# Two PSUM banks for the transposes between the stages of a two-block transformer, and an urgent half of the modulation

## The chip, the cores and the metric

The kernel runs on one core of a Trainium2 chip, in one launch. The metric is the device time of an execution in microseconds. A core has five engines that each work through their own fixed list of instructions: TensorE (PE: matmuls and transposes; PEld is its loading of weights), VectorE (DVE), ScalarE (ACT), GpSimd (POOL) and SyncE (SP, which issues the loads). They wait for each other by semaphores. Matmul results land in PSUM, which has eight banks of 2 KB for each of 128 partitions.

## What is computed

Two blocks over 256 tokens of 1024 features, in float32. The first is an mLSTM mixer (with a context of 256 more tokens) followed by a gated convolution MLP; the second has two layers, each with three sublayers: feed-forward, mixer (gated linear attention in the first layer, latent attention in the second), feed-forward. What concerns this change is how every sublayer begins: the tokens are normalised and each feature is scaled and shifted by numbers that depend on the conditioning vector `c`.

```python
def rmsnorm_2(x, g):
    xf = x.astype(jnp.float32)
    y = xf * lax.rsqrt(jnp.mean(xf * xf, axis=-1, keepdims=True) + EPS)
    return (y * g.astype(jnp.float32)).astype(x.dtype)

def swiglu(h, w_gu, w_down):
    gate, up = jnp.split(h @ w_gu, 2, axis=-1)
    return (jax.nn.silu(gate) * up) @ w_down

def sublayer(x, shift, scale, gate, g_pre, g_post, fn, res_weight):
    h = rmsnorm_2(x, g_pre) * (1 + scale[:, None, :]) + shift[:, None, :]
    return x + res_weight * gate[:, None, :] * rmsnorm_2(fn(h), g_post)
```

## The kernel before

Tokens are worked on in two halves of 128, called t = 0 and t = 1 here, features in eight groups of 128. The weights (340 MB of traffic in all) are streamed from HBM once, 512 KB at a time (`raw`), and every float32 product is made of three matmuls: each operand is split into a rounded part and its remainder, and `mm3` (lines 250 to 252) sums hi x hi, hi x lo and lo x hi. For a weight ScalarE makes the rounded part (`whi`, line 236, or `wA`, `wB`, `wC` where it has a place of its own) and VectorE the remainder (`wlo`, line 237). For the activations ScalarE makes `u_hi` and VectorE `u_lo` (`hilo`, lines 245 and 246). VectorE also works off a queue of background products of the conditioning vector with weights (`gjunk`, line 256).

Between two stages stands this chain, once for each token half: the squares are summed (ScalarE, `ajunk`, line 324), VectorE forms the root in some five small operations (lines 298 to 311), and scales the tokens to `xn` (line 370, or 908 at the start of the first feed-forward). In `modulated` TensorE transposes `xn` by groups of four features into one PSUM bank (`pt`, line 347, tag `tc`); for the first four groups VectorE applies scale and shift (`u`, line 358), for the last four ScalarE does (line 362); then each half of `u` is split into `u_hi` and `u_lo`. The bank holds one half: the transposes of the second half wait until the first four modulations have read it. `modulated` is called 16 times: twice each at the start of the gated convolution MLP, the four feed-forwards apart from the one at the layer boundary, the gated linear attention and the latent attention, and four times at the boundary of the two layers, where two differently modulated copies are made of each token half.

The tag `tr` of the same pool is a second bank with one buffer. The feed-forward uses it for the transposes of its product `h_` (`pt2`, line 966), the helper `row_of` for a row vector, the attention parts for their own transposes.

The program is written as a plain sequence; a scheduler sorts each engine's list at build time by its own estimate of when things are ready and by priority. `urgent(offset)` raises the priority of what is issued in it: the ends of stages are written inside such blocks (`with urgent(uo(t)): fin(t, acc)`), with matmuls of the stage that ends or of the other token half as work to put between. So an edit in `modulated` can move instructions that it doesn't name. In the feed-forward the order of chunk products is a list (`FFN_ORDER`), whose accumulators are `acc`, and whose up products land in `mm`.

Of the kernel before, what the change touches and what calls it, by code (L numbers as in the profile page):

```python
# [7 lines left out]
F32 = mybir.dt.float32  # L8
# [4 lines left out]
ALU = mybir.AluOpType  # L13
# [97 lines left out]
def kernel(ctx: ExitStack, tc: tile.TileContext, a: dict, out: bass.AP):  # L111
    nc = tc.nc
    V, S, T, G = nc.vector, nc.scalar, nc.tensor, nc.gpsimd

    def pool(name, bufs, **kw):
        return ctx.enter_context(tc.tile_pool(name=name, bufs=bufs, **kw))
# [14 lines left out]
    ps_tr = pool("ps_tr", 1, space=PSUM)  # L131

    def urgent(offset=1500):
        return tc.high_priority(offset=offset)
# [109 lines left out]
    def hilo(hi, lo, src):  # L244
        mark["ehi"] = S.copy(hi, src)  # L245
        mark["elo"] = V.tensor_tensor(out=lo, in0=src, in1=hi.bitcast(F32), op=ALU.subtract)  # L246
        return mark["elo"]
# [95 lines left out]
    def t4(src, h, pt=None):  # L343
        if pt is None:
            pt = ps_tr.tile([128, 4, 128], F32, name="pt", tag="tc")
        for k in range(4):
            T.transpose(pt[:, k, :], src[:, (h * 4 + k) * 128:(h * 4 + k + 1) * 128], ident)  # L347
        return pt

    def modulated(xn, gs, sh, uh, ul):  # L350

        for h in range(2):
            ks = slice(h * 4, h * 4 + 4)
            pt = t4(xn, h)
            u = wk.tile([128, 4, 128], F32, name="u", tag="u")
            if h == 0:
                for k in range(4):
                    V.tensor_scalar(out=u[:, k, :], in0=pt[:, k, :], scalar1=gs[:, k:k + 1], scalar2=sh[:, k:k + 1],
                                    op0=ALU.mult, op1=ALU.add)
            else:  # L360
                for k in range(4):
                    S.activation(out=u[:, k, :], in_=pt[:, k, :], func=AF.Identity,
                                 scale=gs[:, 4 + k:5 + k], bias=sh[:, 4 + k:5 + k])
            hilo(uh[:, ks, :], ul[:, ks, :], u)
# [8 lines left out]
    def prenorm(src, gs, sh, t):  # L373
        ts = slice(t * 128, t * 128 + 128)
        xn = normed(src)
        modulated(xn, gs, sh, u_hi[:, :, ts], u_lo[:, :, ts])
        return xn
# [508 lines left out]
    def fin_glu(t, acc):  # L886
        ga2, gfin = rows1
        y = wk.tile([128, D], F32, name="y", tag="xn")
        ss = sm.tile([128, 8], F32, name="ssf", tag="ssf", bufs=2)
        for h, v in enumerate(halves(y)):  # L890
            s = slice(h * 512, h * 512 + 512)
            V.tensor_tensor(out=v, in0=acc[h], in1=ga2[:, s], op=ALU.mult)
            V.tensor_tensor(out=v, in0=x[:, t, s], in1=v, op=ALU.add)
            mean_square(v, ss[:, h:h + 1], D)
        z = x[:, t, :]
        for h, v in enumerate(halves(y)):
            w = z[:, h * 512:h * 512 + 512]
            V.tensor_tensor(out=w, in0=v, in1=gfin[:, h * 512:h * 512 + 512], op=ALU.mult)
            mean_square(w, ss[:, 2 + h:3 + h], D)
        V.tensor_scalar(out=ss[:, 4:5], in0=ss[:, 0:1], scalar1=ss[:, 1:2], scalar2=0.5 * EPS, op0=ALU.add, op1=ALU.add)  # L900
        V.tensor_scalar(out=ss[:, 5:6], in0=ss[:, 2:3], scalar1=ss[:, 3:4], scalar2=None, op0=ALU.add)
        r = rsqrt_half(ss[:, 4:5])
        V.tensor_scalar(out=ss[:, 6:7], in0=ss[:, 5:6], scalar1=r, scalar2=r, op0=ALU.mult, op1=ALU.mult)
        V.tensor_scalar(out=ss[:, 6:7], in0=ss[:, 6:7], scalar1=0.5 * EPS, scalar2=None, op0=ALU.add)
        r2 = rsqrt_half(ss[:, 6:7])
        xn = wk.tile([128, D], F32, name="xn", tag="xn")
        for v, w in zip(halves(xn), halves(z)):
            V.tensor_scalar(out=v, in0=w, scalar1=r, scalar2=r2, op0=ALU.mult, op1=ALU.mult)
        ts = slice(t * 128, t * 128 + 128)
        modulated(xn, mod2[:, 1, :], mod2[:, 0, :], u_hi[:, :, ts], u_lo[:, :, ts])  # L910
        V.tensor_scalar_mul(out=z, in0=z, scalar1=r)
# [275 lines left out]
    def mla_u(t, xn):  # L1187

        if t == 0:
            mla.u = second()  # L1190
        ts = slice(t * 128, t * 128 + 128)
        modulated(xn, mod2[:, 19, :], mod2[:, 18, :], mla.u[0][:, :, ts], mla.u[1][:, :, ts])
# [310 lines left out]
```

## Time and profile before

| | |
|---|---|
| median of 3 runs | 1437.48 us (1434.57 to 1437.93) |
| the profiled execution | 1434.38 us |
| its span, first to last instruction | 1432.6 us |
| mean granted clock of TensorE | 0.986 of full |
| TensorE busy | 1380.0 us, 96% |
| VectorE busy | 1113.9 us, 78% |
| ScalarE busy | 720.5 us, 50% |
| data moved | 340.24 MB, 238 GB/s in the mean |

In the rows further down, a line of the timeline gives an operation's start and its length in microseconds, engine and source line, what it writes and reads, how many are taken together (x4), and in brackets how long the engine had been idle before it and what ended that. A waiting row gives the engine that waited, the instruction it waited at, what it waited for, and the sum, the number and the longest of such waits. Matmuls overlap: each takes 0.39 us at full clock though the next starts 0.23 us after it.

### The profile page before, as it was taken

The page shows a single profiled execution, that of the slowest core. Times are in us where ns is not written, and L with a number is a line of the kernel's source. Part 1 is how long each engine was busy: PE and PEld are TensorE (multiplying, and loading weights), DVE is VectorE, ACT ScalarE, POOL GpSimd, SP SyncE. Part 2 cuts the span into 40 slices and gives each one's busy share as a digit, 9 for nine tenths or more (in the row PEclk, how much of TensorE's full clock was granted, in tenths as well). Part 3 has the DMA queues.
Part 4 walks back from the last instruction along what each step waited for, and adds up shares of the span by engine and source line. Part 5 has one row for each costly group of instructions (what it writes and reads, how often), then busy time and mean ns, then how long its engine had stood idle before and what let it go on. Part 6 is the DMA issues. An engine that isn't in the chain of part 4 may idle for free.

```text
span 1432.6 us, 22526 instructions
## 1 busy us (share of the span) xinstructions
PE 1380.0 (96%) x8425; PEld 1204.0 (84%) x8425; DVE 1113.9 (78%) x2115; ACT 720.5 (50%) x1188; POOL 18.2 (1%) x42
## 2 busy tenths in 40 slices
PE   6999999999989999999999999999999999899997
PEld 6978877899978999878678999879999776789996
DVE  6887788898688888689788888698878786756563
ACT  4634764545354545566454545554554666644451
POOL 1000000000000000000000000000000000000000
PEclk8999999999999999999999999999999999999999
DMA  8576446797528999568548999469889472366750
GB/s 330 203 265 234 162 151 234 264 323 272 184 96 290 336 340 345 196 222 290 187 154 289 341 335 344 147 202 334 317 310 333 138 253 80 121 198 205 276 170 30
DMA packets 94943, 340.24 MB, mean 238 GB/s; under 512 B 10928, under 2 KB 11248, under 8 KB 94832
## 3 DMA queue, kind: packets, MB, share of 16 engines
q1 hardware_dynamic: 92736, 332.47, 65.6%
q0 software_dynamic: 2096, 6.33, 1.5%
q8 instruction: 66, 1.08, 0.3%
q14 instruction: 45, 0.37, 0.1%
HBM read 337.67 MB, written 1.08 MB: 236 GB/s over the span
## 4 chain that ended last, share of the span: by engine, by line
PE 70%; DVE 11%; DMA 10%; ACT 4%; issue 3%; SPq 0%; DVEq 0%; ACTq 0%; POOLq 0%
PE mm L250 12%; PE mm L252 11%; PE mm L251 11%; PE acc L252 8%; PE acc L250 8%; PE acc L251 8%; DMA raw<-in_cond_w_dram 3%; DVE wlo L237 3%; DVE gjunk L256 2%; PE acc L733 2%; ACT whi L236 1%; ACT ajunk L324 1%; PE pt L347 1%; PE pg L556 1%; DMA row<-d 1%
## 5 line engine op out<-in xcount | busy, mean ns | idle before, releaser
L237 DVE TENSOR_TENSOR wlo<-raw,whi 128x1024 fp32r<-128x1024 f32 (+1 forms) x385 | 462.5, 1207 | 109.6 <-ACT whi L236 106.7
L236 ACT CAST whi<-raw 128x1024 fp32r<-128x1024 f32 (+1 forms) x385 | 395.7, 1038 | 277.1 <-PE mm L251 79.5
L250 PE MATMUL mm<-u_hi,whi 128*128 128x256 f32 x1384 | 388.5, 281 | 0.2 <-DVE hf L831 0.2
L251 PE MATMUL mm<-u_lo,whi 128*128 128x256 f32 x1384 | 386.6, 279 | 0.0
L252 PE MATMUL mm<-u_hi,wlo 128*128 128x256 f32 x1384 | 386.5, 279 | 0.0
L250 PEld LDWEIGHTS mm<-u_hi,whi 128*128 128x128 f32 x1384 | 260.0, 188 | 4.4 <-DVE hf L831 0.6
L251 PEld LDWEIGHTS mm<-u_lo,whi 128*128 128x128 f32 x1384 | 259.3, 187 | 3.3
L252 PEld LDWEIGHTS mm<-u_hi,wlo 128*128 128x128 f32 x1384 | 260.1, 188 | 0.0
L256 DVE CUSTOM_DVE_ANT_0 gjunk<-raw,c 128x1024 bf16<-128x1024 f32 x192 | 234.3, 1221 | 24.1 <-DMA raw<-in_cond_w_dram 16.5
L250 PE MATMUL acc<-whi,hh 128*128 128x512 f32 x388 | 153.6, 398 | 4.5 <-ACT hh L245 4.5
L252 PE MATMUL acc<-whi,hl 128*128 128x512 f32 x388 | 153.3, 397 | 0.3 <-DVE hl L246 0.3
L251 PE MATMUL acc<-wlo,hh 128*128 128x512 f32 x388 | 152.5, 393 | 0.5 <-DVE wlo L237 0.5
L252 PEld LDWEIGHTS acc<-whi,hl 128*128 128x128 f32 x388 | 73.4, 189 | 17.4 <-DVE hl L246 0.7
L250 PEld LDWEIGHTS acc<-whi,hh 128*128 128x128 f32 x388 | 72.9, 188 | 17.5 <-ACT hh L245 5.0
L252 PE MATMUL acc<-whi,u_lo 128*128 128x512 f32 (+1 forms) x216 | 86.7, 403 | 0.5 <-DVE u_lo L246 0.5
L250 PE MATMUL acc<-whi,u_hi 128*128 128x512 f32 (+1 forms) x216 | 86.5, 401 | 0.0
L251 PE MATMUL acc<-wlo,u_hi 128*128 128x512 f32 (+1 forms) x216 | 86.4, 400 | 0.0
L251 PEld LDWEIGHTS acc<-wlo,hh 128*128 128x128 f32 x388 | 73.2, 189 | 14.2 <-DVE wlo L237 1.3
L251 PE MATMUL mm<-wlo,u_hi 128*128 128x512 f32 x144 | 57.3, 398 | 0.0
L250 PE MATMUL mm<-whi,u_hi 128*128 128x512 f32 x144 | 57.2, 397 | 0.0
L252 PE MATMUL mm<-whi,u_lo 128*128 128x512 f32 x144 | 57.0, 397 | 0.0
L946 ACT ACTIVATE sg<-mm 128x256 f32<-128x256 f32 x64 | 24.3, 380 | 59.6 <-PE mm L252 59.5
(734 smaller groups left out, 1998.6 us busy)
## 6 DMA issues: line engine op xcount, KB each, us to landing
raw<-in_cond_w_dram SPq DMA_DIRECT2D x144, 512.0 KB, 5.2
raw<-in_gu_ws_dram SPq DMA_DIRECT2D x128, 512.0 KB, 5.0
raw<-in_dn_dram SPq DMA_DIRECT2D x88, 512.0 KB, 4.9
raw<-in_gu_dram SPq DMA_DIRECT2D x48, 512.0 KB, 4.3
raw<-in_w_mod_dram SPq DMA_DIRECT2D x32, 512.0 KB, 4.3
raw<-in_f_down_dram SPq DMA_DIRECT2D x22, 512.0 KB, 4.6
raw<-in_f_gate_dram SPq DMA_DIRECT2D x18, 512.0 KB, 4.9
raw<-in_a_vo_dram SPq DMA_DIRECT2D x16, 512.0 KB, 5.1
```

The source lines that it names most:

```text
L236: o1 = S.copy(hi[:, :n], r[:, :n])
L237: o2 = V.tensor_tensor(out=lo[:, :n], in0=r[:, :n], in1=hi[:, :n].bitcast(F32), op=ALU.subtract)
L250: T.matmul(ps, lhsT=lh, rhs=rh, start=first, stop=False)
L251: T.matmul(ps, lhsT=lh, rhs=rl, start=False, stop=False)
L252: T.matmul(ps, lhsT=ll, rhs=rh, start=False, stop=last)
L256: return V.tensor_tensor_reduce(out=junk, in0=r, in1=vec, scale=1.0, scalar=0.0, op0=ALU.mult, op1=ALU.add, accum_out=dst)
L324: mark["ms"] = S.activation(out=junk[:, :src.shape[-1]], in_=src, func=AF.Square, scale=float(2 * width) ** -0.5, accum_out=dst)
L347: T.transpose(pt[:, k, :], src[:, (h * 4 + k) * 128:(h * 4 + k + 1) * 128], ident)
L556: o = T.matmul(pg, lhsT=wsc[:, k * 128:k * 128 + 128], rhs=ccol[:, k, :], start=(k == 0), stop=(k == 7))
L733: T.matmul(np_[:, 0:257], lhsT=w[:, d, s, :], rhs=vt[s][:, h, :], start=(i == 0), stop=(i == len(tiles) - 1))
L946: S.activation(out=sg, in_=ps[:, 0:256], func=AF.Silu)
```

## The change

In `modulated` the transposes of both halves are issued first, the first half's into `tc` as before, the second half's into `tr`; VectorE's four modulations stand in `urgent(2500)`, above the offsets of 300 to 2000 used elsewhere in the kernel. Two lines are added, so line 358 of before is 360 after, 362 is 364, 908 is 910, and so on.

```diff
@@ -349,14 +349,16 @@
 
     def modulated(xn, gs, sh, uh, ul):
 
+        pts = [t4(xn, 0), t4(xn, 1, ps_tr.tile([128, 4, 128], F32, name="pt", tag="tr"))]
         for h in range(2):
             ks = slice(h * 4, h * 4 + 4)
-            pt = t4(xn, h)
+            pt = pts[h]
             u = wk.tile([128, 4, 128], F32, name="u", tag="u")
             if h == 0:
-                for k in range(4):
-                    V.tensor_scalar(out=u[:, k, :], in0=pt[:, k, :], scalar1=gs[:, k:k + 1], scalar2=sh[:, k:k + 1],
-                                    op0=ALU.mult, op1=ALU.add)
+                with urgent(2500):
+                    for k in range(4):
+                        V.tensor_scalar(out=u[:, k, :], in0=pt[:, k, :], scalar1=gs[:, k:k + 1], scalar2=sh[:, k:k + 1],
+                                        op0=ALU.mult, op1=ALU.add)
             else:
                 for k in range(4):
                     S.activation(out=u[:, k, :], in_=pt[:, k, :], func=AF.Identity,
```

The lists of SyncE and GpSimd stay as they are. Those of TensorE, VectorE and ScalarE move at every call. Three places follow, all at the start of the first feed-forward.

VectorE before, ahead of the second token half's norm result `xn` (four `wlo` stand between the previous half's `u_lo` and `xn`; `h__4310` is a product of the feed-forward that has begun on the first token half, `hl` its remainder):

```order
L308 SCALAR_TENSOR_TENSOR w<-w 128x1
L237 TENSOR_TENSOR wlo<-raw,whi 128x1024
L309 SCALAR_TENSOR_TENSOR r<-w,yi 128x1
L237 TENSOR_TENSOR wlo<-raw,whi 128x1024
L310 SCALAR_TENSOR_TENSOR w<-r,ssf 128x1
L237 TENSOR_TENSOR wlo<-raw,whi 128x1024
L311 SCALAR_TENSOR_TENSOR r<-w,r 128x1
L237 TENSOR_TENSOR wlo<-raw,whi 128x1024
L908 TENSOR_SCALAR xn<-x,r 128x512 x2
L963 TENSOR_TENSOR h__4310<-sg,mm 128x256
L911 TENSOR_SCALAR x<-x,r 128x1024
L358 TENSOR_SCALAR u<-pt,mod_118 128x128 x4
```

VectorE after, from that product on; five `wlo` stand already ahead of the first row here:

```order
L965 TENSOR_TENSOR h__4310<-sg,mm 128x256
L311 SCALAR_TENSOR_TENSOR r<-w,r 128x1
L256 ISA gjunk,mod_118<-raw,c_2574 128x1024
L256 ISA mod_118 128x1
L905 TENSOR_SCALAR ssf<-ssf,r 128x1
L237 TENSOR_TENSOR wlo<-raw,whi 128x1024
L906 TENSOR_SCALAR ssf<-ssf 128x1
L237 TENSOR_TENSOR wlo<-raw,whi 128x1024
L298 TENSOR_SCALAR yi<-ssf 128x1
L306 TENSOR_SCALAR w<-ssf 128x1
L307 SCALAR_TENSOR_TENSOR w<-yi,w 128x1
L237 TENSOR_TENSOR wlo<-raw,whi 128x1024
```

and straight on:

```order
L308 SCALAR_TENSOR_TENSOR w<-w 128x1
L965 TENSOR_TENSOR h__4370<-sg,mm 128x256
L309 SCALAR_TENSOR_TENSOR r<-w,yi 128x1
L310 SCALAR_TENSOR_TENSOR w<-r,ssf 128x1
L311 SCALAR_TENSOR_TENSOR r<-w,r 128x1
L910 TENSOR_SCALAR xn<-x,r 128x512 x2
L913 TENSOR_SCALAR x<-x,r 128x1024
L360 TENSOR_SCALAR u<-pt,mod_118 128x128 x4
```

Between the previous half's `u_lo` and `xn` are now eight `wlo`, one `gjunk` and the products `h__4310` and `h__4370`; before there were four `wlo` and nothing of the others.

TensorE before, around the two sets of transposes of the same token half (`mm` are up products of the first token half, `mm<-wA,u_hi` the first of the second):

```order
L252 MATMUL mm<-whi,u_lo 128x512
L347 MATMUL pt<-ident,xn 128x128 x4
L250 MATMUL mm<-whi,u_hi 128x512
L966 MATMUL pt_4312<-ident,h__4310 128x128 x2
L251 MATMUL mm<-wlo,u_hi 128x512
```

and, six matmuls on,

```order
L252 MATMUL mm<-whi,u_lo 128x512
L250 MATMUL mm<-whi,u_hi 128x512
L347 MATMUL pt<-ident,xn 128x128 x4
L250 MATMUL acc_4258<-whi,hh 128x512
L250 MATMUL acc_4259<-whi,hh 128x512
L250 MATMUL mm<-wA,u_hi 128x512
L251 MATMUL mm<-wA,u_hi 128x512
```

TensorE after, the same place:

```order
L250 MATMUL mm<-whi,u_hi 128x512
L251 MATMUL mm<-wlo,u_hi 128x512
L252 MATMUL mm<-whi,u_lo 128x512
L347 MATMUL pt<-ident,xn 128x128 x8
L968 MATMUL pt_4312<-ident,h__4310 128x128 x2
L250 MATMUL mm<-wA,u_hi 128x512
L251 MATMUL mm<-wA,u_hi 128x512
L250 MATMUL acc_4258<-whi,hh 128x512
L251 MATMUL acc_4258<-wlo,hh 128x512
L252 MATMUL mm<-wA,u_lo 128x512
```

The ten matmuls on `whi` that stood between the two sets, and five more that came behind the first of the new token half, are ahead of both; the feed-forward's transpose `pt_4312` follows the eight, and the first matmul of the new token half follows that.

ScalarE before, at the first token half (`ajunk` are sums of squares of the other half's norm):

```order
L236 CAST wC<-raw 128x1024
L236 CAST wA<-raw 128x1024
L324 ACTIVATE ajunk,ssf<-y 128x512 x2
L324 ACTIVATE ajunk,ssf<-x 128x512 x2
L245 CAST u_hi<-u 128x4x128
L362 ACTIVATE u<-pt,mod_118 128x128 x4
L245 CAST u_hi<-u 128x4x128
L236 CAST whi<-raw 128x1024 x5
```

ScalarE after, the same place:

```order
L236 CAST wC<-raw 128x1024
L364 ACTIVATE u<-pt,mod_118 128x128 x4
L245 CAST u_hi<-u 128x4x128 x2
L236 CAST wA<-raw 128x1024
L236 CAST whi<-raw 128x1024
L324 ACTIVATE ajunk,ssf<-y 128x512
L236 CAST whi<-raw 128x1024
L324 ACTIVATE ajunk,ssf<-y 128x512
```

The four modulations come before both casts of `u_hi`, and both of those before the sums of squares, which are now apart from each other with casts of weights between.

## Rows read from the trace of the kernel before

**Rows 1.** The page, busy time, share of the span and number of instructions.

```profile
PE 1380.0 (96%) x8425; PEld 1204.0 (84%) x8425; DVE 1113.9 (78%) x2115; ACT 720.5 (50%) x1188; POOL 18.2 (1%) x42
```

**Rows 2.** Waits of TensorE: us in total, times, longest us.

```profile
PE pt L347 <- DVE u L358: 8.6, 6, 3.6
...
PE pt L347 <- DVE xn L370: 5.1, 4, 2.4
...
PE mm L250 <- ACT u_hi L245: 0.2, 1, 0.2
```

**Rows 3.** Timeline, start of the gated linear attention, second token half.

```profile
622.47 0.66 PE L347 MATMUL pt<-ident,xn 128*128 128x128 f32 x4 [0.81 <-DVE xn L370]
623.16 1.36 DVE L358 TENSOR_SCALAR u<-pt,mod 128x128 f32<-128x128 f32 x4 [0.35 <-PE pt L347]
...
624.56 0.62 ACT L245 CAST u_hi<-u 128x512 fp32r<-128x512 f32 x1 [1.50 <-DVE u L358]
...
624.58 0.66 PE L347 MATMUL pt<-ident,xn 128*128 128x128 f32 x4 [1.46 <-DVE u L358]
...
625.23 0.58 PE L250 MATMUL mm<-u_hi,whi 128*128 128x256 f32 x1
625.27 1.51 ACT L362 ACTIVATE u<-pt,mod 128x128 f32<-128x128 f32 x4
...
628.07 2.35 DVE L237 TENSOR_TENSOR wlo<-raw,whi 128x1024 fp32r<-128x1024 f32 x2
```

**Rows 4.** Timeline, first feed-forward, first token half: VectorE, then TensorE.

```profile
413.03 1.04 DVE L358 TENSOR_SCALAR u<-pt,mod 128x128 f32<-128x128 f32 x3
414.05 1.38 DVE L892 TENSOR_TENSOR y<-acc,row 128x512 f32<-128x512 f32 x2
...
417.87 0.40 DVE L358 TENSOR_SCALAR u<-pt,mod 128x128 f32<-128x128 f32 x1
...
418.31 1.21 DVE L237 TENSOR_TENSOR wA<-raw,wA 128x1024 fp32r<-128x1024 f32 x1
...
418.32 1.12 PE L347 MATMUL pt<-ident,xn 128*128 128x128 f32 x4 [3.63 <-DVE u L358]
...
420.19 0.63 PE L251 MATMUL mm<-wA,u_hi 128*128 128x512 f32 x1
```

**Rows 5.** Windows: TensorE's busy us (instructions), granted clock, share of DMA, GB/s.

```profile
418.00:421.00 3.00, 2.52 (x7) 0.50 0.14 34
421.00:425.00 4.00, 4.00 (x13) 0.66 0.36 119
...
625.00:628.00 3.00, 3.00 (x11) 0.52 0.39 137
...
1234.00:1237.00 3.00, 2.93 (x9) 0.50 0.02 5
```

**Rows 6.** Timeline, first feed-forward, second token half: VectorE, ScalarE, TensorE.

```profile
427.50 1.00 DVE L908 TENSOR_SCALAR xn<-x,r 128x512 f32<-128x512 f32 x2
428.41 0.41 DVE L963 TENSOR_TENSOR h__4310<-sg,mm 128x256 f32<-128x256 f32 x1
...
434.06 1.22 DVE L256 CUSTOM_DVE_ANT_0 gjunk<-raw,c 128x1024 bf16<-128x1024 f32 x1
...
429.85 1.05 ACT L236 CAST whi<-raw 128x1024 fp32r<-128x1024 f32 x1 [2.10 <-DMA raw<-in_dn_dram]
...
429.27 0.60 PE L347 MATMUL pt<-ident,xn 128*128 128x128 f32 x4
...
431.10 0.40 PE L252 MATMUL mm<-whi,u_lo 128*128 128x512 f32 x1
431.34 0.39 PE L250 MATMUL mm<-whi,u_hi 128*128 128x512 f32 x1
...
432.26 0.60 PE L347 MATMUL pt<-ident,xn 128*128 128x128 f32 x4
```

**Rows 7.** Timeline of TensorE, last feed-forward, first token half.

```profile
1234.07 1.11 PE L347 MATMUL pt<-ident,xn 128*128 128x128 f32 x4 [1.52 <-DVE u L358]
```

## The prediction

> **What bounds the kernel now.** I read the busy line of the page first: TensorE works 1380.0 of 1432.6 us [rows 1], so only its 52.6 us of idle time and the stretches at half clock can move the end. Then I asked for the waits of TensorE. Two of its groups belong to this code: the second set of transposes (line 347) waited for VectorE's modulations `u` (line 358) six times, 8.6 us in all, 3.6 us the longest, and the first set waited for the norm's result `xn` four times, 5.1 us. The matmuls waited for ScalarE's cast `u_hi` once, 0.2 us [rows 2]. The 8.6 us are everything that a second bank can take away directly, 0.6% of the span. Then I looked at single places in the timeline.
>
> A stage begins so, in the gated attention's second half of the tokens [rows 3]: four transposes at 622.47, VectorE's four modulations from 623.16 (1.36 us), TensorE idle for 1.46 us, the other four transposes at 624.58 (they need the bank that VectorE has just emptied), beside them the cast `u_hi` of the first half (0.62 us), and at 625.23 the first matmul. From the first transpose to the first matmul are 2.76 us. ScalarE's modulations of the second half (1.51 us) come only then. The first matmul takes features from the first half, so the first cast decides.
>
> The longest wait stands at the start of the first feed-forward layer, first token half [rows 4]: VectorE runs three modulations from 413.03, then six operations of the other token half's norm (lines 892, 893 and 898, from 414.05 on), and only then the fourth at 417.87. TensorE resumes at 418.32. Its matmul of line 251 there, at 420.19, needs VectorE's `wA` (418.31 to 419.5).
>
> The windows give the granted clock behind such waits [rows 5]: 0.50 from 418 to 421 (the lower of the two levels, 1.2 GHz), a mixture of both to 425 at 0.66, 0.52 from 625 to 628, 0.50 from 1234 to 1237. Busy time at a clock c holds c as much work, so the place at 418 cost 2.52 x 0.50 + 4.00 x 0.34 = 2.6 us, that at 625 3.00 x 0.48 = 1.4 us, and that at 1234 2.93 x 0.50 = 1.5 us in this window.
>
> **What the change does at any site.** It adds no instruction and no transfer; the order of SyncE and GpSimd does not move, so no load is issued elsewhere in the program. Eight transposes go back to back and take 1.2 us (0.66 for four, 0.13 more for each of the next four [rows 3]). VectorE and ScalarE then modulate at the same time, from different banks. What is late next is ScalarE: in its fixed order the four modulations of half 1 stand ahead of both casts, as the order of ScalarE in the section on the change shows for the first feed-forward start. So the first matmul comes at 1.2 + 1.51 + 0.62 = about 3.4 us from the first transpose, where before it came at 2.76: 0.65 us later, though the second half's features are there 1 us earlier. An idle TensorE is not idle for less; its wait goes over from `u` to `u_hi`. Where matmuls of the old stage stand between, the 3.4 us are covered if there are nine or more of them (2.1 us beside the 1.2 us of transposes).
>
> The Trainium skill (Perfetto Trace Analysis, Matmuls) says that independent groups should rotate through different PSUM banks so that the evacuation of one overlaps the next group's matmuls. By that rule alone the 8.6 us would go, and the time would be the gain rival's below. The trace here shows what stands behind the bank, a cast on an engine that has just been given two jobs ahead of it.
>
> **First feed-forward start, first token half.** The fourth modulation now follows the third, at 414.05, and the 3.63 us stall in front of the transposes goes. But VectorE still owes six norm operations (3.8 us, from 414.05 to the fourth modulation [rows 4]), two `u_lo` (half a `wlo` in elements, some 0.6 us each) and `wA` (1.15), in that order: 414.4 + 3.8 + 1.2 + 1.15 = 420.5 us. The matmul of line 251 needs that and started at 420.19 before. I take +0.3 us; the bounds are -3.6 (the whole wait goes) and +1.
>
> **First feed-forward start, second token half.** This is the largest term. Before, VectorE had four `wlo` between the `u_lo` and this half's `xn`, which ran from 427.50 to 428.4, and TensorE reached the transposes at 429.27 without waiting [rows 6]. After, by VectorE's order, eight `wlo`, one `gjunk` and the two products `h__4310` and `h__4370` stand ahead of `xn`: 4 x 1.13 + 1.15 + 2 x 0.35 = 6.4 us more (the second `wlo` of a pair adds 1.13 of 2.35 [rows 3]; `gjunk` and `h` by rows 6, less the overlap of some 0.07), so `xn` is whole at about 434.8. It can be later: the last of these `wlo` need feed-forward weights whose `whi` casts ScalarE could start only at 429.85, after waiting 2.10 us for the transfer; two more at some 2 us each make it 437. TensorE meanwhile has run out: the ten matmuls on `whi` that stood between the two sets of transposes and five that came soon after are now all ahead of the first (429.27 + 15 x 0.23 = 432.7, the pitch by rows 6; with the 0.3 from above 433.0). That is a hole of 1.8 us, 4 if the transfers bind; I take the first. Behind it the eight transposes, then at once the feed-forward's own transpose `pt_4312`, whose bank is now the one that ScalarE empties, and the first matmul: 3.4 less 1.3 = 2 us more that nothing covers, where before there was no gap at all. Two holes so near each other have gone with half clock at each of the three places of rows 5, at 1.4 to 2.6 us each; I count 2.5. Sum 1.8 + 2 + 2.5 = +6.3 us, bounds 0 (VectorE runs ahead of what I think) and +9.
>
> **Gated attention start.** First token half: TensorE's order has only three matmuls after the eight transposes, then a feed-forward transpose that waits for ScalarE's modulations, and the first projection; before, seven stood between the sets and a gap of 0.25 us was all. I take +1.4. Second half: `xn` as before; 0.65 us later by the site rule, less the 0.81 us that TensorE waited for `xn` [rows 3] if the first hole delays it enough. The half-clock stretch of 625 may stay or go (1.4). Together +0.7, bounds -3 and +2.
>
> **The other twelve calls.** The start of the convolution part has 18 and 11 covering matmuls behind the transposes and costs nothing; the latent attention's start has 12 and 15 and costs nothing. At the layer boundary the second token half has four sets of transposes in a row where before they were apart; the last feed-forward's first half exchanges its 1.52 us [rows 7] for about the same. Its second half loses the matmuls that covered it and gets a hole of some 1.7 us; the second feed-forward's second half gets 0.8. Less what later waits of TensorE absorb I take +2 of these 2.5, bounds -3 and +5.
>
> The sum is 0.3 + 6.3 + 0.7 + 2 = +9.3 us on the profiled execution's 1434.4 (its span and 1.8 around it), 1443.7. That execution is 3.1 us below the median of the runs and within 0.2 us of the fastest, so 1444 is less of a loss against the median than against itself: +6.5, 0.45%.
>
> **The rivals.** Gain: the 8.6 us go, and with them two of the three slow stretches (2.6 and 1.4). Time: 1437.5 - 12.6 = 1425, or 1429 if only the waits go. For it: the 3.63 us at 418 are really an order fault, which the urgency mends; against it: line 251 still waits for `wA`. No change: each `u` wait becomes a `u_hi` wait of the same length and the later `xn` is covered, because the loads let VectorE work ahead: 1437 within 4. Worse than forecast: bank `tr` is shared with every feed-forward transpose, so each start also holds up the finished products, and slow clock follows at the second halves of all three feed-forward starts (the two more at 2 to 2.6 us, and their holes at 2 to 3: 10 us): 1454. It decides where the feed-forward's own transpose stands between these transposes and the first matmul, as at three places. That the change does not do what it says is excluded by the order of TensorE: the eight transposes stand together at all sites.
>
> **How the numbers follow.** A difference under 0.3%, 4.3 us, cannot be told from none here. Forecast (with the worse case in the same sign): 0.62, of which 0.08 is the worse case. No change: 0.18. Gain: 0.20. The range goes from 1433, which leaves the larger part of the gain out, to 1456; the forecast's own range is 1440 to 1452.
>
> **What would show it.** In the profile after: the wait of the second transposes for `u` gone from TensorE's list; in its place the first matmuls waiting for `u_hi` and some tenths to 3 us of waits for `xn`; a TensorE hole near 433 to 437 with the clock at about 0.5 behind it. If `xn` of the second token half ends before 432 there, the largest term is wrong. If ScalarE's cast comes before TensorE needs it at the gated attention's start, the site rule is wrong.

## The result, and the profile after

The changed kernel takes 1455.36 us (median of 5 runs, 1452.94 to 1459.44), the kernel before 1436.20 us beside it (5 runs, 1434.17 to 1437.93): a ratio of 1.0142, 95% interval 1.0123 to 1.0161. The direction of the forecast was right and its size less than half of what came: 1444 was forecast, 6.5 us over the kernel before, and the medians lie 19.2 us apart. 1455.36 lies beyond the forecast's own range of 1440 to 1452, and inside the wide one of 1433 to 1456, which takes in the rival "worse than forecast" (1454). The profiled execution took 1452.94 us against 1434.38 before.

The page after, busy line:

```profile
PE 1385.9 (96%) x8425; PEld 1208.7 (83%) x8425; DVE 1115.5 (77%) x2115; ACT 720.2 (50%) x1188; POOL 18.2 (1%) x42
```

The instruction counts are those of [rows 1], so the same work is done. TensorE is busy 5.9 us more, though it executes the same matmuls: that part I put down to the slower clock (a mean granted clock of 0.980, 0.986 before). The span is 18.5 us longer, so some 12.6 us are new idle time. The waits of TensorE after (in total, times, longest us) say where to look:

```profile
PE pt L347 <- DVE xn L372: 10.9, 8, 8.5
...
PE pt L968 <- ACT u L364: 4.7, 4, 1.6
PE mm L250 <- ACT u_hi L245: 3.8, 4, 1.5
...
PE pt L347 <- DVE u L360: 2.1, 2, 1.1
```

Against [rows 2], the 8.6 us behind `u` fell to 2.1, as the change means. But `u_hi` rose from 0.2 to 3.8, a wait of the feed-forward's own transposes (line 968, 966 before) for ScalarE's `u` appears with 4.7, and a single wait for `xn` of 8.5 us stands at the top. Line 372 serves most sites, so the group doesn't say which one; the timeline does: it is the boundary of the two layers.

Landmarks divide the 18.5 us. Where TensorE begins the same transposes in both traces (us):

| transposes of | before | after | difference | between them |
|---|---|---|---|---|
| `xn`, first feed-forward, t = 0 | 412.01 | 410.99 | -1.0 | |
| `h__6111` (end of that feed-forward) | 593.78 | 600.54 | +6.8 | +7.8: first feed-forward |
| `h__9429` (end of layer 0) | 912.04 | 920.06 | +8.0 | +1.3: gated attention, second feed-forward |
| `h__11739` (end of layer 1's first) | 1117.35 | 1136.16 | +18.8 | +10.8: layer boundary |
| `h__14838` (last) | 1419.51 | 1438.08 | +18.6 | -0.2: latent attention, last feed-forward |

Of the boundary's 10.8 us, 9.3 have come by the transposes of `h__9916`, a product early in the new feed-forward (964.37 before, 981.67 after).

**The first feed-forward.** The timeline after, first token half, TensorE and VectorE:

```profile
415.79 0.51 PE L250 MATMUL mm<-wA,u_hi 128*128 128x512 f32 x1 [1.62 <-ACT wA L236]
...
418.30 0.80 PE L250 MATMUL mm<-whi,u_hi 128*128 128x512 f32 x1 [2.00 <-ACT whi L236]
418.43 1.22 DVE L237 TENSOR_TENSOR wA<-raw,wA 128x1024 fp32r<-128x1024 f32 x1
...
419.70 0.80 PE L251 MATMUL mm<-wA,u_hi 128*128 128x512 f32 x1 [0.60 <-DVE wA L237]
```

The 3.63 us behind the fourth modulation [rows 4] became 1.62 + 2.00 + 0.60 = 4.22 us: two waits for casts of weights, which ScalarE now makes after its modulations, and one for VectorE's remainder of `wA`. The same for the second half:

```profile
427.83 0.42 DVE L965 TENSOR_TENSOR h__4310<-sg,mm 128x256 f32<-128x256 f32 x1 [1.17 <-ACT sg L963]
...
432.35 0.40 PE L252 MATMUL mm<-whi,u_lo 128*128 128x512 f32 x1
...
434.45 1.00 DVE L910 TENSOR_SCALAR xn<-x,r 128x512 f32<-128x512 f32 x2
435.05 1.12 PE L347 MATMUL pt<-ident,xn 128*128 128x128 f32 x8 [2.31 <-DVE xn L910]
...
437.76 0.60 PE L968 MATMUL pt<-ident,h__4310 128*128 128x128 f32 x2 [1.60 <-ACT u L364]
438.93 0.80 PE L250 MATMUL mm<-wA,u_hi 128*128 128x512 f32 x1 [0.57 <-ACT u_hi L245]
```

Before, TensorE crossed this place without a gap [rows 6]. After, it ends its last covering matmul at 432.75, waits 2.31 us for `xn`, then 1.60 for ScalarE to empty the bank that `pt_4312` needs, then 0.57 for the cast. `h__4310`, whose transpose that is, had been whole since 428.25, 9.5 us earlier.

**The layer boundary.** Before, around the first token half's sets (TensorE, VectorE):

```profile
923.81 0.41 DVE L963 TENSOR_TENSOR h__9602<-sg,mm 128x256 f32<-128x256 f32 x1
...
924.28 0.44 PE L966 MATMUL pt<-ident,h__9602 128*128 128x128 f32 x2 [0.25 <-DVE h__9602 L963]
924.78 0.60 PE L347 MATMUL pt<-ident,xn 128*128 128x128 f32 x4
...
929.41 1.32 DVE L921 TENSOR_TENSOR y<-acc,row 128x512 f32<-128x512 f32 x2
...
937.88 0.38 PE L966 MATMUL pt<-ident,h__9760 128*128 128x128 f32 x2
...
947.25 0.66 PE L347 MATMUL pt<-ident,xn 128*128 128x128 f32 x4
```

and after:

```profile
931.83 0.41 DVE L965 TENSOR_TENSOR h__9602<-sg,mm 128x256 f32<-128x256 f32 x1
...
932.70 1.11 PE L347 MATMUL pt<-ident,xn 128*128 128x128 f32 x8 [0.18 <-DVE xn L372]
...
940.14 0.49 ACT L364 ACTIVATE u<-pt,mod 128x128 f32<-128x128 f32 x1
940.82 0.38 PE L968 MATMUL pt<-ident,h__9602 128*128 128x128 f32 x2
...
945.26 1.28 DVE L923 TENSOR_TENSOR y<-acc,row 128x512 f32<-128x512 f32 x2
...
950.35 0.40 PE L252 MATMUL mm<-whi,u_lo 128*128 128x512 f32 x1
...
959.22 1.97 PE L347 MATMUL pt<-ident,xn 128*128 128x128 f32 x8 [8.48 <-DVE xn L372]
...
968.18 0.38 PE L968 MATMUL pt<-ident,h__9760 128*128 128x128 f32 x2
```

`h__9602` is the last product of the old feed-forward, for t = 1. It is whole at 932.24 but transposed only at 940.82, 8.6 us later, since the two calls for t = 0 have asked for the bank `tr` ahead of it and ScalarE empties the second one at 940.63. Before it waited 0.06 us. What comes behind it is late too: the last down products of t = 1, its post-norm (`y`, 12.6 us after the first set where it was 4.6), and at the end `xn`: the first set of t = 1 follows the first set of t = 0 by 26.5 us (959.22 - 932.70), by 22.5 before (947.25 - 924.78). That is 4.0 us. Further, the new feed-forward's own first products stand behind too: `h__9760` is transposed at 968.18, after all sets of t = 1, where it was at 937.88, ahead of them. Before, 18 `acc` matmuls of the new feed-forward (4.1 us at a pitch of 0.23) lay between 942.1 and the first set and covered the wait for `xn`. After, TensorE is out of work at 950.75. The later `xn` and the lost cover, 4.0 + 4.1 us, make 8.1 of the 8.48 us.

The clock then takes its share (windows after: busy us of TensorE with instructions, its weight loads, VectorE, ScalarE, GpSimd, granted clock, share of DMA, GB/s):

```profile
436.00:440.00 4.00, 1.83 (x7) 1.09 (x6) 3.84 (x9) 2.92 (x7) 0.00 (x0) 0.74 0.51 204
440.00:444.00 4.00, 4.00 (x12) 3.15 (x11) 0.96 (x3) 0.37 (x1) 0.00 (x0) 0.50 0.35 122
...
959.00:963.00 4.00, 2.65 (x11) 2.25 (x12) 3.23 (x10) 1.77 (x5) 0.00 (x0) 0.50 0.63 200
963.00:967.00 4.00, 4.00 (x14) 3.40 (x13) 2.72 (x7) 3.06 (x8) 0.00 (x0) 0.50 0.15 62
```

From 959 to 967 TensorE works 6.65 us at the lower level, 1.2 GHz, after having stood idle; at full clock that would be 3.3 us. Before, the stretch from 950 to 958 was granted 1.00.

### The profile page after: what moved, and what is told of

It is laid out like the page before. It is cut to its first block, busy times and chain, and to the rows that moved or that the text cites. A ratio compares the mean times of both kernels' runs of the same rounds, so it can differ in the third digit from the quotient of the medians.

```text
span 1451.1 us, 22543 instructions
## 1 busy us (share of the span) xinstructions
PE 1385.9 (96%) x8425; PEld 1208.7 (83%) x8425; DVE 1115.5 (77%) x2115; ACT 720.2 (50%) x1188; POOL 18.2 (1%) x42
## 4 chain that ended last, share of the span: by engine, by line
PE 71%; DVE 11%; DMA 8%; ACT 6%; issue 3%; SPq 0%; DVEq 0%; ACTq 0%
PE mm L250 12%; PE mm L252 12%; PE mm L251 12%; PE acc L250 9%; PE acc L252 8%; PE acc L251 8%; DVE wlo L237 3%; ACT whi L236 2%; DMA raw<-in_cond_w_dram 2%; DVE gjunk L256 2%; PE acc L735 2%; ACT ajunk L324 1%; PE pg L558 1%; ACT u L364 1%; DMA raw<-in_gu_ws_dram 1%
## 5 line engine op out<-in xcount | busy, mean ns | idle before, releaser
L251 PEld LDWEIGHTS acc<-wlo,u_hi 128*128 128x128 f32 x216 | 40.6, 188 | 10.4 <-issue 2.1
```

The costliest lines, as they stand in the source:

```text
L251: T.matmul(ps, lhsT=lh, rhs=rl, start=False, stop=False)
```

## The experiments

Each kernel below has both forms of `modulated`; two tuples say at which of its 16 calls the second bank and the urgency are on. (The first two runs are plain edits of `modulated` that leave out one half of the change; their tuples say what the edit amounts to.) The calls are, in the program's order, 0 and 1 the convolution part, 2 and 3 the first feed-forward (t = 0, t = 1), 4 and 5 the gated attention, 6 and 7 the second feed-forward, 8 and 9 the boundary for t = 0 (two copies), 10 and 11 the boundary for t = 1, 12 and 13 the latent attention, 14 and 15 the last feed-forward.

```diff
+        pts = [t4(xn, 0), t4(xn, 1, ps_tr.tile([128, 4, 128], F32, name="pt", tag="tr"))] if n in BANKS else None
...
-            pt = t4(xn, h)
+            pt = pts[h] if pts else t4(xn, h)
...
+                with (urgent(2500) if n in URG else nullcontext()):
```

Ratios are to the kernel before, run beside each on the same chip, with 95% intervals; where a difference in us is given for a run, it is the ratio's on 1434 us. By that measure the whole change costs 20.4 us (19.2 by the medians, the figure that some expectations use).

**Which half of the change does it?** Banks in all calls, no urgency:

```diff
+BANKS, URG = range(16), ()
```

> The two banks without the raised urgency of VectorE's modulations. Theory (the second bank does it): the lists of TensorE are those of the changed kernel, and VectorE's differ from them only in some ten rows at the last feed-forward's start; ratio to before 1.013 to 1.015, within 3 us of the changed kernel. Rival (the urgency pushes the norms back): ratio under 1.007, with the 8.5 us hole of the layer boundary gone.

Measured: 1458.36 us, 1.0174 (1.0153 to 1.0195). That is above the 1.013 to 1.015 that I expected, and the rival is refuted: the banks alone cost more than the whole change, by 0.0032 with about 0.0028 either way. The longest hole is that of the kernel after, at the same place, and there 8.48 us:

```profile
957.50 1.97 PE L347 MATMUL pt<-ident,xn 128*128 128x128 f32 x8 [8.59 <-DVE xn L371]
```

Urgency in all calls, one bank:

```diff
+BANKS, URG = (), range(16)
```

> The raised urgency with the one bank of before. Theory: at the layer boundary the norm of the second token half stands where it did, so no hole near 950 us; at the first feed-forward's second half the fourth modulation comes early, `u_lo` with it, and seven `wlo` slip ahead of `xn`, so a hole of 2 to 4 us stays there; ratio 1.002 to 1.006 (3 to 9 us). Rival (the urgency does it): 1.010 or more. Second rival (the second bank does all of it): 1.000, within 2 us.

Measured: 1429.34 us, 0.9968 (0.9951 to 0.9986), faster than both kernels; my expectation of a loss is refuted. The timeline of its first feed-forward, one line of the first token half, then the second:

```profile
418.06 0.79 PE L251 MATMUL mm<-wA,u_hi 128*128 128x512 f32 x1 [3.15 <-DVE wA L237]
...
427.26 0.38 PE L967 MATMUL pt<-ident,h__4310 128*128 128x128 f32 x2
...
431.41 1.00 DVE L909 TENSOR_SCALAR xn<-x,r 128x512 f32<-128x512 f32 x2
...
432.00 0.66 PE L347 MATMUL pt<-ident,xn 128*128 128x128 f32 x4
432.42 0.48 PE L250 MATMUL acc<-whi,hh 128*128 128x512 f32 x1
...
435.24 0.60 PE L347 MATMUL pt<-ident,xn 128*128 128x128 f32 x4
```

`xn` of t = 1 is late here too: its list of VectorE has seven `wlo`, a `gjunk` and a product ahead of it, much as after the change. Counted from the first set of t = 0, `xn` starts 21.4 us later (431.41 - 410.06), by 15.5 before and by 23.5 after the change. Yet TensorE doesn't stop. It reaches the first set just as `xn` is there, and between the two sets stand twelve down products (`acc`), from 432.42 to 435.24. They are not the ten up products that stood there before; those are ahead of both sets, as after the change. The down products can stand there because `h__4310`, which they need, was transposed at 427.26, as soon as it was whole. After the change its transpose comes at 437.76, behind the sets. So with the urgency alone `xn` is 2.1 us less late than after the change, and the feed-forward's own product isn't held up; no run parts the two.

**How much is each place?** The change at the first feed-forward alone:

```diff
+BANKS, URG = (2, 3), (2, 3)
```

> Before, with two banks and urgency at the first feed-forward's start alone. Theory (splits of weights slip in front of the second half's norm, and the ten covering matmuls stand ahead of the transposes): the holes of the changed kernel at 435 to 439 us come back one for one, 6 to 8 us, ratio 1.004 to 1.0055. Rival (the loss of the changed kernel is all at the layer boundary): within 2 us.

Measured: 1444.78 us, 1.0064 (1.0043 to 1.0085), 9.2 us, above the expected 1.004 to 1.0055, which reaches into the interval; the rival is refuted. The holes of the second token half are those after the change (2.31 and 1.60 us):

```profile
438.26 1.97 PE L347 MATMUL pt<-ident,xn 128*128 128x128 f32 x8 [2.31 <-DVE xn L918]
441.82 0.69 PE L976 MATMUL pt<-ident,h__4310 128*128 128x128 f32 x2 [1.59 <-ACT u L371]
```

The change at the boundary, for t = 0 alone and for t = 1 alone (everything else as before):

```diff
+BANKS, URG = (8, 9), (8, 9)
```

> Before, with two banks and urgency at the layer boundary's first token half alone (two of the sixteen calls). Theory (the bank `tr` is taken twice ahead of the old feed-forward's last transpose `h__9602`, which makes the second half's norm late): TensorE transposes `h__9602` some 8 us after it is ready, a hole of about 8 us waits for `xn`, and the time is 9 to 12 us over before, ratio 1.006 to 1.008. Rival (the cast chain of four uncovered sets at the second half): 0 to 2 us.

```diff
+BANKS, URG = (10, 11), (10, 11)
```

> Before, with two banks and urgency at the layer boundary's second token half alone. Theory: `h__9602` is transposed at once and `xn` comes as before; the site costs 0 to 2 us, ratio 1.000 to 1.0015. Rival (the cast chain of four uncovered sets): 8 us or more, ratio above 1.005.

Measured: t = 0 1440.68 us, 1.0047 (1.0032 to 1.0062), 6.7 us, less than expected (the hole is 3.18 us, not 8); t = 1 1437.80 us, 1.0025 (1.0009 to 1.0041), 3.6 us, more than expected. I had put nearly all on t = 0. The sum, 10.3 us, is near the boundary's 10.8; how far that is luck is said in the last section. The trace with t = 0 alone:

```profile
921.56 0.42 DVE L973 TENSOR_TENSOR h__9602<-sg,mm 128x256 f32<-128x256 f32 x1
...
930.56 0.38 PE L976 MATMUL pt<-ident,h__9602 128*128 128x128 f32 x2
...
948.73 1.11 PE L347 MATMUL pt<-ident,xn 128*128 128x128 f32 x4 [3.18 <-DVE xn L380]
```

and with t = 1 alone:

```profile
935.02 0.41 DVE L973 TENSOR_TENSOR h__9760<-sg,mm 128x256 f32<-128x256 f32 x1
...
944.93 1.94 PE L347 MATMUL pt<-ident,xn 128*128 128x128 f32 x8 [4.79 <-DVE xn L380]
...
956.35 0.38 PE L976 MATMUL pt<-ident,h__9760 128*128 128x128 f32 x2
```

These are two different harms. With t = 0 alone the old feed-forward's last transpose comes 8.6 us late (921.98 to 930.56), and t = 1's first set follows t = 0's (at 922.42) by 26.3 us where it was 22.5. With t = 1 alone that distance is 22.0 us, so `xn` is on time, but the new feed-forward's product, whole at 935.4, is transposed at 956.35, behind the sets, and TensorE runs out of work ahead of them.

The change everywhere else:

```diff
+BANKS, URG = (0, 1, 4, 5, 6, 7, 12, 13, 14, 15), (0, 1, 4, 5, 6, 7, 12, 13, 14, 15)
```

> The change in the ten calls outside the first feed-forward of layer 0 and the layer boundary, the kernel before in those six. Theory (the change's 19.2 us are 9.1 at that feed-forward and 10.3 at the boundary, the rest nothing): 1434 to 1439 us, a ratio of 0.999 to 1.002. Rival (my prediction's +2 lies spread over the other calls, the gated attention's start above all): 1.002 to 1.005.

Measured: 1439.25 us, 1.0015 (0.9999 to 1.0031). The interval leaves out neither theory; at most 4.5 us lie there. With 9.2 and 10.3 the three parts make 21.7 us against the 20.4 of the whole, each run known to 2 or 3 us.

**Is it the place in the queue for the bank?** The calls at the boundary take another bank (`mm`) instead of `tr`; all other calls are as after the change (line shortened):

```diff
+pts = [t4(xn, 0), t4(xn, 1, mm_ps() if n in (8, 9, 10, 11) else ps_tr.tile(...))]
```

> The changed kernel, with the second half's transposes at the four calls of the layer boundary put into a bank of the two that the products `mm` use, instead of `tr`. Theory (the boundary's loss is that `tr` is held ahead of the old and the new feed-forward's own transposes, which hold up the sums that the norm and TensorE's covering work need): `h__9602` is transposed within 3 us of being ready, the wait for `xn` at the second half falls from 8.5 to under 4 us, and the time is 5 to 9 us under the changed kernel, ratio to before 1.007 to 1.011. Rival (two engines working at once, and the cast after them, cost it, whichever bank): 1.014, unchanged.

Measured: 1468.06 us, 1.0225 (1.0204 to 1.0246), which neither theory had. The trace:

```profile
943.94 0.41 DVE L973 TENSOR_TENSOR h__9602<-sg,mm 128x256 f32<-128x256 f32 x1
944.41 0.44 PE L976 MATMUL pt<-ident,h__9602 128*128 128x128 f32 x2 [1.43 <-DVE h__9602 L973]
...
959.94 1.12 PE L347 MATMUL pt<-ident,xn 128*128 128x128 f32 x4 [10.12 <-DVE xn L380]
```

`mm` is where the old feed-forward's last product is summed, so now the product itself is whole only at 944.35. The same harm, one step earlier; the run doesn't part the theories, it shows that no bank here is idle.

So the order was changed instead of the bank. In the old feed-forward the last up projection (t = 1) is written ahead of the last down projection of t = 0, which lets its transpose ask for `tr` before the boundary's calls. This was run with the change and, as a control, without it:

```diff
-        seq = FFN_ORDER
+        seq = list(FFN_ORDER)
+        if (l, j) == (0, 1):
+            seq[-4], seq[-3] = seq[-3], seq[-4]
```

> The changed kernel, with one more edit at the layer boundary alone: in the old feed-forward (layer 0, second) the last up projection of token tile 1 is put into the program ahead of the last down projection of token tile 0, so that the old feed-forward's last transpose asks for the bank `tr` before the t0 calls of the modulation do. Theory (the boundary's cost is the place in the queue for the one bank `tr`): the last transpose of the old feed-forward stands ahead of the sets again, its 8.6 us of delay and with them the late xn of t1 go, and the boundary costs 3 to 6 us where it cost 10.8: a ratio of 1.008 to 1.012 to before. Rival (the banks cost by holding PE's sequencer at the sets, wherever the old transposes stand): no change against the changed kernel, 1.013 to 1.016.

> The control of the exchange: the kernel before with the same exchange of the last up and down projection in the old feed-forward, and nothing of the change. Theory: in the kernel before the last transpose has its bank in time anyway, so the exchange is worth nothing: 0.998 to 1.003. If the exchange gains by itself (a rival for whatever the run before shows), this falls below 0.997, and the other run is to be read against it.

Measured: with the change 1457.20 us, 1.0143 (1.0119 to 1.0166); the control 1442.09 us, 1.0042 (1.0027 to 1.0057). Read alone the first is what the rival expected. But the exchange by itself costs 6.0 us, which I had put at nothing: the last up projection no longer covers the wait for `xn` of t = 0. The control has, at the boundary:

```profile
929.31 0.84 PE L347 MATMUL pt<-ident,xn 128*128 128x128 f32 x4 [3.16 <-DVE xn L380]
...
949.18 0.60 PE L347 MATMUL pt<-ident,xn 128*128 128x128 f32 x4
```

and with the change:

```profile
927.96 0.43 PE L978 MATMUL pt<-ident,h__9488 128*128 128x128 f32 x2
...
938.66 1.11 PE L347 MATMUL pt<-ident,xn 128*128 128x128 f32 x4 [3.15 <-DVE xn L380]
...
959.80 1.97 PE L347 MATMUL pt<-ident,xn 128*128 128x128 f32 x8 [4.09 <-DVE xn L380]
...
970.34 0.38 PE L978 MATMUL pt<-ident,h__9760 128*128 128x128 f32 x2
```

Against the control the change costs 14.5 us (1.0143 - 1.0042) where it costs 20.4 without the exchange. The last transpose (now named `h__9488`) is on time; t = 1's first set follows t = 0's by 21.1 us, 19.9 in the control, so `xn` is 1.3 us late instead of 4.0; and the hole is 4.09 us instead of 8.48. What is left of it is for the larger part the other harm: `h__9760` still stands at 970.34, behind the sets, and with it the `acc` matmuls that it feeds, seven of which stand ahead of the first set in the control. So the two parts of the 8.48 us are seen apart in the traces. The times agree, but weakly: 1.0142 less (1.0143 - 1.0042) is 0.0041, with about 0.0034 either way.

**Where does the urgency gain?** At the last feed-forward's first half alone, and at the first feed-forward alone:

```diff
+BANKS, URG = (), (14,)
```

> Before, with the urgency alone (one bank) at the last feed-forward's first token half alone. Theory (of the urgency's gain nearly all is there, since the four modulations are no longer parted by a norm operation, and the half-clock stretch goes): ratio 0.996 to 0.998. Rival (the gain is at the first feed-forward): 0.999 to 1.001.

```diff
+BANKS, URG = (), (2, 3)
```

> The kernel before with the urgency alone, and that only in the two calls of layer 0's first feed-forward; the second transposes stay in the bank they had. The urgency in all calls measured 0.9968. Theory (its gain is made at that feed-forward, where t0's hole of 3.63 us before the second set becomes shorter and t1's x leaves the filler matmuls between its sets): 0.996 to 0.998, 1430 to 1433 us. Rival (the gain comes from the later calls, at layer 1's second feed-forward or between, or from several places): 0.9985 to 1.001.

Measured: 1434.00 us, 0.9995 (0.9980 to 1.0009), and 1431.93 us, 0.9983 (0.9970 to 0.9997). The first is nothing that can be told, and speaks against what I expected of it. The second would be about half of the gain, between the two theories, and is only just clear of none (0.4 to 4.3 us). Its trace doesn't show the gain at that feed-forward: from the first set of t = 0 to `h__6111` it takes 181.7 us, 181.8 before and 181.8 with the urgency in all calls. Its `h__4310` does come 3.0 us earlier than before (426.93 for 429.94), but in the control of the exchange, where nothing is changed up to there, it comes 2.1 us earlier (427.82). With the urgency in all calls the trace gains at the start of the last feed-forward: from `h__11886` to `h__13082` it takes 111.1 us for 117.8. The last section has what is different there. The urgency at calls 10 and 11 alone was not run, so where the gain lies stays open.

**How far one profile can be trusted.** The rebuilt form with nothing on:

```diff
+BANKS, URG = (), ()
```

> The kernel before with nothing changed in what it does, as a measure of what two runs of one program differ by and of what its profile shows twice. Ratio 1.000 within 0.2%. If the vector that the last post-norm multiplies by lands late again (VectorE's wait of 5.0 us for it before 1221.94), the hole of 2.4 us for `xn` there belongs to the program; if not, it is chance of the transfer, and some 4 us of what the profiles differ by are not the change's.

Measured: 1435.03 us, 0.9999 (0.9984 to 1.0015), so the rebuilt form is the kernel before. But its profiled execution has a span of 1440.7 us against 1432.6, for the same lists of instructions.

## Why the prediction was wrong in size

**The first feed-forward, t = 0: right.** Forecast +0.3; its three waits sum to 4.22 us for 3.63, +0.6. `wA` is whole at 419.65 where I had worked out 420.5; as the stage begins 1.0 us earlier after the change, that is 8.7 us behind its first set for 8.5. I had named VectorE's `wA` as what comes last; casts on ScalarE (1.62 and 2.00 us) take most of the time, which I had not listed.

**The first feed-forward, t = 1: right in its terms, with one cause not seen.** `xn` whole at 434.8 forecast, 435.45 measured; TensorE out of work at 433.0 forecast, 432.75 measured; a hole of 1.8, measured 2.31; the chain behind it 2, measured 1.60 + 0.57; clock 2.5, measured 2.5 (0.5 from 436 to 440 and 2.0 from 440 to 444). Counted from the stage's earlier beginning, `xn` was 1.7 us later than forecast and TensorE's last work 0.8, which partly cancel in the hole. The stage comes out at +7.8 by the landmarks and 9.2 alone, for 6.6 forecast. What I left out is in the run with the urgency: down products could have stood between the sets and behind them, had `h__4310` not waited 9.5 us for its turn at the bank.

**The site rule: right on the wait, not on the 0.65 us.** An idle TensorE does wait for `u_hi` or the bank instead: 1.53 us for `u_hi` at the gated attention's second half (it waited 0.81 and 1.46 [rows 3]), 1.53 at the last feed-forward's first half (1.52 [rows 7]), and 1.60 for the bank at its second half, where I had 1.7. From the first transpose to the first matmul I had 3.4 us (my terms sum to 3.33) for 2.76. It measured 2.84 at the gated attention's second half (629.38 to 632.22), and 3.33 at the last feed-forward's first half (1249.90 to 1253.23), which had been 3.63. Gated attention and second feed-forward together: 0.7 + 0.8 forecast, 1.3 measured; the 0.7 is my judgement, the terms beside it don't sum to it.

**The step that failed: the layer boundary, inside "the other twelve calls".** I wrote that "the second token half has four sets of transposes in a row where before they were apart" and then gave the boundary no term at all: the 2.5 us of that paragraph are 1.7 for the last feed-forward's second half and 0.8 for the second feed-forward's, of which I kept 2, with +5 as the upper bound of all twelve calls. It measured 10.8 us in the profile and 10.3 as the sum of two runs. I looked at the sets that stand together and at what follows them in the new stage, and not at who else asks for the bank `tr` meanwhile. The last transpose of the *old* feed-forward stands in that line, and its result is on the path to the next half's norm. The worse rival had the mechanism, "bank `tr` is shared with every feed-forward transpose, so each start also holds up the finished products", and 1454 us, but at another place (the second halves of the three feed-forward starts) and a chance of 0.08. Its condition, where the feed-forward's transpose stands between the sets and the first matmul, was met at three places in the order that I had; I counted the wait at the bank and not what is built on the product that waits. The traces bear this out: with t = 0 alone the last transpose comes 8.6 us late, and with the exchange it is on time and the hole is 4.09 us instead of 8.48. The times bear it out less clearly, since the exchange has a cost of its own.

**No change: refuted** by the first feed-forward alone (1.0064).

**Gain: wrong for the whole, and on the urgency not for its reason.** I said that the 3.63 us at 418 "are really an order fault, which the urgency mends". Alone the urgency does gain, 4.6 us in all, but not those: TensorE waits there 1.22 us for `u_hi` and 3.15 for `wA`, 4.4 in all, as the argument against this rival had it. The 1425 needed the banks to take the `u` waits away at no price.

The Trainium skill (Perfetto Trace Analysis, Matmuls) advises independent groups to rotate through different banks. The waits for `u` did fall from 8.6 to 2.1 us, so the trace agrees on that wait. The rotated bank had other users, and those users lost more: banks alone 1.0174.

## What to carry to other kernels

Before a second buffer is borrowed from a shared pool, list everyone who takes that tag in the stretch between the new request and its release, the stage that is just ending above all, and follow the one that is pushed back to whoever waits for its result. Transposes that are moved together take the work between them along, and a product that is transposed later holds back the matmuls that it feeds: look at what covered the next wait and whether it can still stand there. When a change has two parts, time them apart; here one part gained 0.3% and the other cost 1.7%.

## What the runs showed that was not expected

- One profile of the same lists of instructions differs by 8 us from another: spans 1432.6 (before) and 1440.7 (the rebuilt form with nothing on). Single stretches differ by up to about 3 us: from `h__9916` to `h__11739` it is 153.0 us in the one and 156.3 in the other. So differences of single places between two profiles carry 2 to 3 us; the times of the runs, not the landmarks, carry the sums above.
- At the last feed-forward VectorE waits for a row that is written to memory and read back: 5.00 us before, 6.11 in the rebuilt form. This goes with the program and not with the execution. In all eight traces in which calls 10 and 11 are as before, the row lands 5.6 to 7.3 us after its issue. In all six in which these calls have the second bank, the urgency or both, it lands after 4.3 to 4.5 us, and `y` waits 2.8 us for TensorE instead. Before, with the change at t = 1 of the boundary alone, and after:

```profile
1221.94 1.29 DVE L921 TENSOR_TENSOR y<-acc,row 128x512 f32<-128x512 f32 x2 [5.00 <-DMA row<-d]
```

```profile
1225.76 1.39 DVE L931 TENSOR_TENSOR y<-acc,row 128x512 f32<-128x512 f32 x2 [2.80 <-PE acc L252]
```

```profile
1240.59 1.39 DVE L923 TENSOR_TENSOR y<-acc,row 128x512 f32<-128x512 f32 x2 [2.81 <-PE acc L252]
```

  In the first two the compute engines' lists are the same from 1025 us on, so what makes the row land earlier stays open. But by the traces the change at the boundary also gains something, far from its place: from `h__11886` to `h__13082` the trace with t = 1 alone takes 5.1 us less than before, that with t = 0 alone 0.2 less. So the 3.6 us of t = 1 alone seem to be what is left of a larger loss, it is partly luck that they and t = 0's 6.7 add up to nearly the boundary's 10.8, and the -0.2 us of the last stages may hide a loss of some microseconds.
- The three holes behind 432 (2.31, 1.60 and 0.57 us) and the one hole of 8.48 cost about the same afterwards: 2.5 us of half clock behind 436, 3.3 us behind 959, by the windows.
